# A hybrid decoder layer on one core: modulation blocks as plain fp32, GpSimd's products moved to VectorE, stores from two queues

## The chip, the core and the metric

The kernel runs on one core of one Trainium2 chip. Such a core has TensorE (matmuls), VectorE, ScalarE, GpSimd and SyncE, which here issues DMA transfers; the profile calls them PE, DVE, ACT, POOL and SP. The metric is the device time of one execution in microseconds, as the median of several runs.

## The reference, cut to what matters

One layer of a decoder trunk is applied to a prompt of 1024 tokens and to 8 single-token samples, with 1024 channels, all in fp32:

```python
mod = silu(c) @ w_ada + b_ada
shift, scale, gate = split(mod, 3)
h = rms_norm(x, norm_g) * (1 + scale) + shift
z = h @ w_in                      # 12 groups of columns, 3 branches
...                               # gated linear attention, short convolution, RG-LRU
out = (g1 * y_gla + g2 * y_sc + g3 * y_rg) @ w_out
x = x + gate * out
y = rms_norm(x, final_gain)
```

The layer also returns the new states of the three branches.

## The kernel before

Channels lie on the 128 partitions, in 8 tiles x0 to x7 of 1032 columns (two halves, each with 512 tokens and 4 samples). A large product is made from a split: `hi` is the operand in a reduced fp32 form (F32R), written by ScalarE, `lo` is the rest, which VectorE subtracts (`split`, L158), and three matmuls (hi hi, hi lo, lo hi) take the place of one. `product` (L336) makes seven block products where eight would be plain (`Pair`, `SEQ`), so the activations are kept in the combinations that `make_t` builds.

The beginning is a list of steps in the string `ORDER` (L36). Each name is a function and a number: X loads x, S squares it and adds to the sums of squares on TensorE, L loads a quarter of a modulation block from `w_ada`, R makes the norm factors (`group_rstd`), A multiplies a quarter (`ada_first`), E ends a block (`ada_end`: copy, transposes, `mod_ab`), N multiplies x by the norm factors (`norm_x`), H applies scale and shift (`make_h`), T makes the combinations and their splits (`make_t`), F multiplies one k of the first two products (`first_mm`), W and V load and split a small weight tile, Y and Z another one. Block j of the four modulation blocks gives scale and shift for x j and x j+4, which H, T and F of that j need.

Blocks 0, 2 and 3 are split, with 16 single matmuls for a block, and block 1 is plain fp32, with 8 (`EX`). The norms of x4 to x7 are on GpSimd (`POOL_J`). The affine step of the tokens is on VectorE for x0 to x3 (`AFF_V`) and on ScalarE for the others.

The order in the text is not the order on an engine. A list scheduler decides it when the program is compiled: of the instructions whose inputs and buffers it reckons to be ready, it queues the one that stands first in the text. The queues are then fixed, and an engine waits at the head of its queue. `tc.issue_after` in `ada_first` keeps TensorE's work for the later quarters behind the norm factors.

Then comes the long stream of 48 pairs of weight tiles, with the branches' work put between its matmuls, then the branch projections (`proj`) for three branches of 8 blocks, each with 48 matmuls for either half, and then the output projection with the final norm, in three parts of the columns (`part`: 388, 388 and 256 columns, each with 8 blocks f of 24 matmuls). For each f VectorE adds gate times product to x (L1206), ScalarE squares the sum (`fsq`, L1216) and VectorE adds the squares. At the end of a part a reciprocal root is made, four products scale the part (L1226), on GpSimd for the first two parts, and eight stores write it.

Buffers of 128 x 1032 come from two pools: `res` with 28 and `tmp` with 11. The splits of the merged activations, `mhi` and `mlo`, are in `res` for j below 6 and in `tmp` for 6 and 7. The weights of the output projection for f from 2 on are in `res` as well, as are the operands of the last branch's projection.

Of the kernel before, what the change touches and what calls it, by code (L numbers as in the profile page):

```python
# [7 lines left out]
F32R = mybir.dt.float32r  # L8
U32 = mybir.dt.uint32
AF = mybir.ActivationFunctionType  # L10
OP = mybir.AluOpType

P = 128
# [16 lines left out]
NSNAP = 5  # L30
WRAW, WSPL = 3, 5
AHEAD = 3
EX = (False, True, False, False)
ADA = ("res", "res", "res", "res")
FIRST_AFTER = (0, 2)
ORDER = (  # L36
# [3 lines left out]
AFF_V = (0, 1, 2, 3)  # L40
POOL_J = (4, 5, 6, 7)
RG_IDLE = (6, 1)
CHAIN = (4, 3)

# [32 lines left out]
def build(tc, a):  # L77
    nc = tc.nc
    from contextlib import ExitStack
    with ExitStack() as ctx:  # L80
# [8 lines left out]
        def bt(tag, name, dt=F32):  # L89
            return bigp.tile([P, TT], dt, name=name, tag=tag, bufs={"res": NRES, "tmp": NTMP}[tag])  # L90
# [19 lines left out]
        def tok(t):  # L110
            return hv(t)[:, :, :TH]
# [17 lines left out]
        vec, act, pe, gp, sp = nc.vector, nc.scalar, nc.tensor, nc.gpsimd, nc.sync  # L129
# [28 lines left out]
        def split(raw, hi, lo):  # L158
            act.activation(hi, raw, AF.Copy)  # L159
            vec.tensor_sub(lo, raw, hi.bitcast(F32))  # L160
# [33 lines left out]
        modA = ct([P, KT, 9], "modA")  # L194
# [5 lines left out]
        def ada_mm(blk, t, ws, i=None, kk=None):  # L200
            pg = ada_st[blk]
            m = 9 if len(ws) == 1 else 20
            for kk in range(2) if kk is None else (kk,):
                k = 2 * t + kk
                for i_ in range(len(ws)) if i is None else (i,):
                    c = csl if m == 9 else (c20, c20h)[i_]
                    pe.matmul(pg[:m], c[:, k, :], ws[i_][kk],  # L207
                              start=(k == 0 and i_ == 0), stop=(k == KT - 1 and i_ == len(ws) - 1))
# [3 lines left out]
        def ada_evac(blk, m):  # L212
            adar[blk] = tmp("adar")[:20, :512]
            act.activation(adar[blk][:m], ada_st[blk][:m], AF.Copy)

        def ada_tr(blk, m, i):
            pe.matmul(ada_st[blk][:, 9 * i:9 * i + 9], adar[blk][:m, i * P:(i + 1) * P], sel[:m], start=True, stop=True)
# [31 lines left out]
                              start=(k == 1 and g == 0), stop=(k == KT - 1 and g == 7))  # L249

        def norm_x(j):
            (gp if j in POOL_J else vec).tensor_mul(xt[j], xt[j], rs["rstd"])

        def make_h(j):
            x = xt[j]
            vec.tensor_mul(smp(x), smp(x), hs(modA[:, j, 1:9]))
            vec.tensor_add(smp(x), smp(x), hs(modB[:, j, 1:9]))
            if j in AFF_V:
                vec.tensor_scalar(tok(x), tok(x), modA[:, j, 0:1], modB[:, j, 0:1], op0=OP.mult, op1=OP.add)
            else:  # L260
                act.activation(tok(x), tok(x), AF.Identity, bias=modB[:, j, 0:1], scale=modA[:, j, 0:1])


        hop, b1a = {}, {}
# [17 lines left out]
                    hop[ids[i], k] = (half(hi, i), half(lo, i))  # L282

        def ada_load(blk, t):
            w = bt(ADA[blk], "wada")
            sp.dma_start(w[:, :1024], a["w_ada"][blk, t])
            raws[blk, t] = w[:, :1024]

        def ada_first(blk, t):
            if t == 0:  # L290
                ada_st[blk] = gpt("ada")
            raw = raws[blk, t]
            with ExitStack() as order:
                if (blk, t) >= FIRST_AFTER:
                    order.enter_context(tc.issue_after(rs["v"]))
                    order.enter_context(tc.issue_after(rs["p"]))
                if EX[blk]:
                    ws = (raw,)
                else:
                    ws = tuple(bt("res", f"ada{blk}_{t}{x}", F32R)[:, :1024] for x in "hl")  # L300
                    split(raw, *ws)
                ada_mm(blk, t, [(w[:, :512], w[:, 512:]) for w in ws])

        def ada_end(blk):
            m = 9 if EX[blk] else 20
            ada_evac(blk, m)
            for i in range(4):
                ada_tr(blk, m, i)
            mod_ab(ada_pt(blk), blk)

        def masks():
# [736 lines left out]
                loaded.add(n)  # L1048
                pairs[n].load()

        rg_consts()
        for q, (p, i) in enumerate(ops):
            n = q // 7
            if q % 7 == 0:
                load(n + 1)
            for d in range(1, AHEAD + 1):
                prep(q + d)
            if n or i not in (1, 2):
                p.mm(i)
            p.post(i)  # L1060
            if q % 7 == 6:
                after(*PAIRS[n])
# [78 lines left out]
        mhi, mlo = [], []  # L1141
        for br in range(3):
            nxt = []
            for j in range(8):
                g = tmp("gl")
                sp.dma_start(g, gs[br][j])
                for h, y in proj(a["wb"][br, j], [t[0] for t in u], [t[1] for t in u], f"y{br}_{j}"):
                    vec.tensor_mul(half(g, h), y, half(g, h))  # L1148
                if br:
                    p0 = tmp("p0")  # L1150
                    sp.dma_start(p0, pps[br - 1][j])
                    vec.tensor_add(g, g, p0)
                if br < 2:
                    sp.dma_start(pps[br][j], g)
                    nxt.append(load_u(br + 1, j, "tmp" if br == 0 and j >= 6 else "res"))
                else:
                    tag = "res" if j < 6 else "tmp"
                    mh, ml = bt(tag, f"mhi{j}", F32R), bt(tag, f"mlo{j}", F32R)
                    split(g, mh, ml)
                    mhi.append(mh)  # L1160
                    mlo.append(ml)
            u = nxt
# [13 lines left out]
        for ci in range(3):  # L1176
            w, wp = part(ci)[1:]

            def view(t):

                if ci == 2:
                    return hv(t)[:, :, :P]
                return part(ci)[0](t)

            def own(t):
                return hv2(t) if ci == 2 else t

            def hv2(t):
                return t.rearrange("p (h n) -> p h n", h=2)

            acc = tmp("facc")
            yp = []
            for f in range(8):
                ps = next_slot("wo_ps")
                o = ps[:, :w]
                for k in range(KT):
                    whi, wlo = (x[k // 4][:, k % 4 * P:(k % 4 + 1) * P] for x in wo[f])
                    for i, (m, x) in enumerate(((whi, mhi[k]), (whi, mlo[k]), (wlo, mhi[k]))):
                        pe.matmul(own(o), m, view(x), start=(k == 0 and i == 0), stop=(k == KT - 1 and i == 2))  # L1199
                if f % 2 == 0:  # L1200
                    yt = tmp("yt")[:, :2 * w].rearrange("p (f t) -> p f t", f=2)
                    for ff in range(2):
                        sp.dma_start(own(yt[:, ff]), view(a["x"][f + ff]))
                    yp.append(yt)
                y = yt[:, f % 2]
                vec.scalar_tensor_tensor(y[:, :wp], o[:, :wp], modG[:, f, 0:1], y[:, :wp], op0=OP.mult, op1=OP.add)  # L1206
                if wp < w:
                    t8 = sm([P, NS], "t8")
                    s0 = 1 + HS * (1 - ci)
                    vec.tensor_mul(t8[:, :HS], o[:, wp:], modG[:, f, s0:s0 + HS])  # L1210
                    vec.tensor_add(y[:, wp:w], y[:, wp:w], t8[:, :HS])  # L1211
                if f == 0:
                    act.activation(acc[:, :w], y, AF.Square)
                else:
                    sq = tmp("fsq")
                    act.activation(sq[:, :w], y, AF.Square)  # L1216
                    vec.tensor_add(acc[:, :w], acc[:, :w], sq[:, :w])
                act.activation(y, y, AF.Copy, scale=col("fgain", f))
            pg = gpt("fms")
            pe.matmul(pg[:, :w], ones_d, acc[:, :w], start=True, stop=True)  # L1220
            rst_ = tmp("frs")
            act.activation(rst_[:, :w], pg[:, :w], AF.Sqrt, bias=epsc)
            vec.reciprocal(rst_[:, :w], rst_[:, :w])  # L1223
            for f in range(0, 8, 2):
                y = yp[f // 2]
                (gp if ci < 2 else vec).tensor_mul(y, y, rst_[:, :w].unsqueeze(1).to_broadcast([P, 2, w]))  # L1226
                for ff in range(2):
                    sp.dma_start(view(a["o_y"][f + ff]), own(y[:, ff]))


def _ktile(w):
# [112 lines left out]
```

## Time and profile before

| | |
|---|---|
| device time, median of 3 runs | 1587.34 us (1586.84 to 1591.46) |
| profiled execution | 1590.05 us, with a span of 1588.2 us |
| TensorE busy | 1524.0 us |
| VectorE busy | 1048.2 us |
| ScalarE busy | 738.4 us |
| GpSimd busy | 31.6 us |
| mean granted clock of TensorE | 0.983 |

The profile is of one execution; its span runs from its first to its last instruction, and the device time lies a little above it. The granted clock is a share of full speed: it has two levels, 0.5 (1.2 GHz) and 1.0 (2.4 GHz), and a mean in between tells how long each was granted. A wait is named by who ended it.

### The profile page before, as it was taken

Reading aid. Unit: us, or ns where it says so; the run is one execution under the profiler, and the core shown is the slowest. Engines: PE = TensorE matmul, PEld = TensorE weight load, DVE = VectorE, ACT = ScalarE, POOL = GpSimd, SP = SyncE. Lnnn points to the kernel's source line nnn. Section 1 sums busy time; section 2 is a strip of 40 time slices with the busy share of each in tenths; the row PEclk is TensorE's granted clock in tenths of the full one; section 3 lists DMA queues with packets and bytes.
Section 4 is the critical chain, followed back from the end, with each engine's and each line's share of the span. In section 5 each row is a group of like instructions: output and inputs, shape, how many; then the busy total and the mean of one; then the engine's idle time right before and its main releaser. Section 6 shows DMA issues by size and latency. Waiting matters only on the chain.

```text
span 1588.2 us, 29025 instructions
## 1 busy us (share of the span) xinstructions
PE 1524.0 (96%) x12170; PEld 1485.4 (94%) x12170; DVE 1048.2 (66%) x1731; ACT 738.4 (46%) x1197; POOL 31.6 (2%) x27
## 2 busy tenths in 40 slices
PE   4899999999999999999999999999999999999995
PEld 3489999999999999999999999999999999999995
DVE  7887587695786966767776768676766434444543
ACT  5556356464473735445363545454544311112332
POOL 4000000000000000000000000000000000000011
PEclk8799999999999999999999999999999999999998
DMA  9011422223124122222112121312147666742223
GB/s 359 27 53 39 144 74 101 90 81 124 68 81 137 54 97 67 97 68 88 63 71 80 71 94 42 123 39 106 47 169 290 239 231 213 256 142 79 95 81 94
DMA packets 58145, 177.53 MB, mean 112 GB/s; under 512 B 7166, under 2 KB 17822, under 8 KB 58014
## 3 DMA queue, kind: packets, MB, share of 16 engines
q1 hardware_dynamic: 58014, 175.68, 31.6%
q8 instruction: 95, 1.56, 0.4%
q14 instruction: 36, 0.29, 0.1%
HBM read 132.64 MB, written 43.02 MB: 111 GB/s over the span
## 4 chain that ended last, share of the span: by engine, by line
PE 73%; DVE 14%; issue 5%; ACT 5%; DMA 1%; POOL 1%; POOLq 0%; DVEq 0%; ACTq 0%; SPq 0%
PE y_ps L1098 17%; PE m_c L342 8%; PE bs_c L342 6%; PE m_d L342 4%; PE rg_c L342 3%; PE ch_c L342 3%; PE gg_c L342 3%; PE qk_c L342 3%; PE bs_d L342 3%; PE wo_ps L1199 3%; DVE xc L856 2%; PE qk_d L342 2%; PE ada L207 2%; PE rg_d L342 1%; PE m_b L342 1%
## 5 line engine op out<-in xcount | busy, mean ns | idle before, releaser
L1098 PE MATMUL y_ps<-ul,y_h 128*128 128x256 f32 (+1 forms) x768 | 153.8, 282 | 0.5 <-DVE ul L160 0.5
L1098 PE MATMUL y_ps<-uh,y_l 128*128 128x256 f32 (+1 forms) x768 | 153.9, 282 | 0.0
L1098 PE MATMUL y_ps<-uh,y_h 128*128 128x256 f32 (+1 forms) x768 | 153.7, 282 | 0.0
L1098 PEld LDWEIGHTS y_ps<-ul,y_h 128*128 128x128 f32 x768 | 119.0, 188 | 1.6 <-DVE ul L160 0.9
L1098 PEld LDWEIGHTS y_ps<-uh,y_h 128*128 128x128 f32 x768 | 118.7, 188 | 0.8 <-ACT y_h L159 0.2
L1098 PEld LDWEIGHTS y_ps<-uh,y_l 128*128 128x128 f32 x768 | 118.7, 188 | 0.7
L159 ACT ACTIVATE y_h<-y_r 128x512 fp32r<-128x512 f32 x48 | 30.0, 629 | 131.6 <-PE y_ps L1098 120.6
L1148 DVE TENSOR_TENSOR gl<-y_ps,gl 128x516 f32<-128x516 f32 x48 | 33.2, 694 | 65.7 <-PE y_ps L1098 64.7
L1199 PE MATMUL wo_ps<-mhi,wo_h 128*128 128x388 f32 (+1 forms) x192 | 62.1, 324 | 3.5 <-DVE yt L1206 3.5
L160 DVE TENSOR_TENSOR y_l<-y_r,y_h 128x512 fp32r<-128x512 f32 x48 | 32.9, 688 | 48.0 <-ACT y_h L159 43.9
L1199 PE MATMUL wo_ps<-mlo,wo_h 128*128 128x388 f32 (+1 forms) x192 | 62.7, 327 | 0.3 <-DVE mlo L160 0.3
L1199 PE MATMUL wo_ps<-mhi,wo_l 128*128 128x388 f32 (+1 forms) x192 | 62.0, 323 | 0.0
L160 DVE TENSOR_TENSOR ul<-ul,uh 128x1032 fp32r<-128x1032 f32 x24 | 29.1, 1230 | 28.7 <-ACT uh L159 28.6
L159 ACT ACTIVATE uh<-ul 128x1032 fp32r<-128x1032 f32 x24 | 25.1, 1064 | 42.1 <-DMA ul<-us 36.1
L1226 POOL TENSOR_TENSOR yt<-yt,frs 128x776 f32<-128x776 f32 x8 | 14.6, 1860 | 1472.2 <-DVE frs L1223 1472.2
L1199 PEld LDWEIGHTS wo_ps<-mhi,wo_h 128*128 128x128 f32 x192 | 36.8, 192 | 3.9 <-DVE yt L1206 3.7
L1199 PEld LDWEIGHTS wo_ps<-mlo,wo_h 128*128 128x128 f32 x192 | 36.9, 192 | 0.9 <-DVE mlo L160 0.6
L1199 PEld LDWEIGHTS wo_ps<-mhi,wo_l 128*128 128x128 f32 x192 | 36.8, 192 | 0.3
L1216 ACT ACTIVATE fsq<-yt 128x388 f32<-128x388 f32 (+1 forms) x21 | 10.3, 491 | 53.3 <-DVE yt L1211 33.0
L1206 DVE SCALAR_TENSOR_TENSOR yt<-wo_ps,modG,yt 128x384 f32<-128x384 f32 (+1 forms) x24 | 13.4, 564 | 31.2 <-PE wo_ps L1199 25.1
L856 DVE SCALAR_TENSOR_TENSOR xc<-xp,pk,xc 128x1022 f32<-128x1022 f32 (+2 forms) x24 | 30.6, 1277 | 0.3
L908 ACT ACTIVATE rgt<-rgg,pk 128x344 f32<-128x344 f32 x48 | 24.0, 545 | 14.0 <-PE rgg L907 13.9
(2818 smaller groups left out, 5058.1 us busy)
## 6 DMA issues: line engine op xcount, KB each, us to landing
ul<-us SPq DMA_DIRECT2D x24, 516.0 KB, 5.7
gl<-gs SPq DMA_DIRECT2D x24, 516.0 KB, 4.8
y_r<-wb SPq DMA_DIRECT2D x24, 512.0 KB, 4.3
pps<-gl SPq DMA_DIRECT2D x16, 516.0 KB, 3.5
p<-pps SPq DMA_DIRECT2D x16, 516.0 KB, 5.6
wada<-w_ada SPq DMA_DIRECT2D x16, 512.0 KB, 10.2
gs<-ga SPq DMA_DIRECT2D x12, 516.0 KB, 2.6
gs<-gb SPq DMA_DIRECT2D x12, 516.0 KB, 2.6
```

The source lines that it names most:

```text
L159: act.activation(hi, raw, AF.Copy)
L160: vec.tensor_sub(lo, raw, hi.bitcast(F32))
L207: pe.matmul(pg[:m], c[:, k, :], ws[i_][kk], start=(k == 0 and i_ == 0), stop=(k == KT - 1 and i_ == len(ws) - 1))
L342: pe.matmul(pv(ps, c), m[:, k * P:(k + 1) * P], x[:, slice(*CHUNKS[c])], start=(first and k == 0 and n == 0), stop=(last and k == 3 and n ...
L856: vec.scalar_tensor_tensor(hv(out)[:, :, s:TH], hv(src)[:, :, :TH - s], w(i), hv(out)[:, :, s:TH], op0=OP.mult, op1=OP.add)
L908: act.activation(self.gate[i][:, cs], ps, AF.Sigmoid, bias=col(("rg_ba", "rg_bx")[i], self.n))
L1098: pe.matmul(pv(ps, c), m, half(x, h)[:, slice(*CHUNKS[c])], start=(k == 0 and i == 0), stop=(k == KT - 1 and i == 2))
L1148: vec.tensor_mul(half(g, h), y, half(g, h))
L1199: pe.matmul(own(o), m, view(x), start=(k == 0 and i == 0), stop=(k == KT - 1 and i == 2))
L1206: vec.scalar_tensor_tensor(y[:, :wp], o[:, :wp], modG[:, f, 0:1], y[:, :wp], op0=OP.mult, op1=OP.add)
L1216: act.activation(sq[:, :w], y, AF.Square)
L1226: (gp if ci < 2 else vec).tensor_mul(y, y, rst_[:, :w].unsqueeze(1).to_broadcast([P, 2, w]))
```

## The change

All four modulation blocks are multiplied as plain fp32, with no split (`EX` and the copies for `hi` and `lo` go). All norms are on VectorE, and all affine steps on ScalarE. `ORDER` is another one: block 3 is loaded with the others, the small weight tile is loaded earlier, two norms stand ahead of the end of each block, and T and F of one j stand between the blocks. `rg_consts` moves from ahead of the stream to its operation 70 in the text. `mhi` and `mlo` of j = 6 and 7 are in `res`. The final scaling is on VectorE in all three parts, and of the stores of each part every other one is issued by ScalarE.

```diff
-EX = (False, True, False, False)
-ADA = ("res", "res", "res", "res")
 FIRST_AFTER = (0, 2)
 ORDER = (
-    "X0 S0 X1 S1 X2 S2 X3 S3 X4 S4 X5 S5 X6 S6 X7 S7 L00 L01 L02 L03 L10 L11 L12 L13 L20 L21 L22 "
-    "L23 R A00 A01 A02 A03 E0 A10 A11 A12 A13 E1 W0 V0 L30 L31 L32 L33 N0 H0 N4 H4 T0 F0 A20 A21 "
-    "A22 A23 E2 N1 H1 N5 H5 T1 F1 A30 A31 A32 A33 E3 N2 H2 N6 H6 T2 F2 N3 H3 N7 H7 T3 F3 Y Z")
-AFF_V = (0, 1, 2, 3)
-POOL_J = (4, 5, 6, 7)
+    "X0 S0 X1 S1 X2 S2 X3 S3 X4 S4 X5 S5 X6 S6 X7 S7 L00 L01 L02 L03 W0 L10 L11 L12 L13 L20 L21 L22 L23 L30 L31 "
+    "L32 L33 R A00 A01 A02 A03 N0 N4 E0 H0 H4 V0 T0 N1 N5 F0 A10 A11 A12 A13 E1 H1 H5 T1 N2 N6 F1 A20 A21 A22 A23 "
+    "E2 H2 H6 T2 N3 N7 F2 A30 A31 A32 A33 E3 H3 H7 T3 F3 Y Z")
...
         def norm_x(j):
-            (gp if j in POOL_J else vec).tensor_mul(xt[j], xt[j], rs["rstd"])
+            vec.tensor_mul(xt[j], xt[j], rs["rstd"])
...
-            if j in AFF_V:
-                vec.tensor_scalar(tok(x), tok(x), modA[:, j, 0:1], modB[:, j, 0:1], op0=OP.mult, op1=OP.add)
-            else:
-                act.activation(tok(x), tok(x), AF.Identity, bias=modB[:, j, 0:1], scale=modA[:, j, 0:1])
+            act.activation(tok(x), tok(x), AF.Identity, bias=modB[:, j, 0:1], scale=modA[:, j, 0:1])
...
-                if EX[blk]:
-                    ws = (raw,)
-                else:
-                    ws = tuple(bt("res", f"ada{blk}_{t}{x}", F32R)[:, :1024] for x in "hl")
-                    split(raw, *ws)
-                ada_mm(blk, t, [(w[:, :512], w[:, 512:]) for w in ws])
+                ada_mm(blk, t, [(raw[:, :512], raw[:, 512:])])
...
-        rg_consts()
         for q, (p, i) in enumerate(ops):
             n = q // 7
+            if q == 70:
+                rg_consts()
...
-                    tag = "res" if j < 6 else "tmp"
-                    mh, ml = bt(tag, f"mhi{j}", F32R), bt(tag, f"mlo{j}", F32R)
+                    mh, ml = bt("res", f"mhi{j}", F32R), bt("res", f"mlo{j}", F32R)
...
-                (gp if ci < 2 else vec).tensor_mul(y, y, rst_[:, :w].unsqueeze(1).to_broadcast([P, 2, w]))
+                vec.tensor_mul(y, y, rst_[:, :w].unsqueeze(1).to_broadcast([P, 2, w]))
                 for ff in range(2):
-                    sp.dma_start(view(a["o_y"][f + ff]), own(y[:, ff]))
+                    (sp if ff else act).dma_start(view(a["o_y"][f + ff]), own(y[:, ff]))
```

## Rows read from the trace of the kernel before

**Rows 1.** The page, busy time by engine: us, share of the span, instructions.

```profile
...
PE 1524.0 (96%) x12170; PEld 1485.4 (94%) x12170; DVE 1048.2 (66%) x1731; ACT 738.4 (46%) x1197; POOL 31.6 (2%) x27
...
```

**Rows 2.** Windows: stretch, length, busy us (PE, PEld, DVE, ACT, POOL), clock, DMA, GB/s.

```profile
...
24.40:95.10 70.70, 51.77 (x224) 29.92 (x224) 65.14 (x97) 39.39 (x51) 14.35 (x5) 0.78 0.28 103
95.10:145.10 50.00, 48.27 (x389) 47.81 (x390) 36.12 (x79) 28.23 (x51) 0.00 (x0) 0.97 0.19 64
...
```

**Rows 3.** Timeline of VectorE and GpSimd from 24 us: start, us, instruction.

```profile
...
25.61 3.40 DVE L160 TENSOR_TENSOR ada_0l<-wada,ada_0h 128x1024 fp32r<-128x1024 f32 x1
...
39.24 3.51 DVE L252 TENSOR_TENSOR x<-x,rstd 128x1032 f32<-128x1032 f32 x3
...
24.50 13.40 POOL L252 TENSOR_TENSOR x<-x,rstd 128x1032 f32<-128x1032 f32 x4 [19.70 <-ACT rstd L333]
...
```

**Rows 4.** Waits from 1480 us: who waited for whom, us, times, longest.

```profile
...
ACT fsq L1216 <- POOL yt L1226: 10.4, 2, 6.1
...
PE wo_ps L1199 <- DVE yt L1206: 3.5, 1, 3.5
...
```

**Rows 5.** Groups of VectorE, shapes apart, 24 to 96: busy us, mean ns.

```profile
...
L160 DVE TENSOR_TENSOR t34l<-t,t34h 128x1032 fp32r<-128x1032 f32 x4 | 4.9, 1226 | 0.0
...
L259 DVE TENSOR_SCALAR x<-x,modA,modB 128x1024 f32<-128x1024 f32 x4 | 3.2, 805 | 0.0
...
L272 DVE TENSOR_TENSOR t<-x,t 128x516 f32<-128x516 f32 x4 | 2.8, 688 | 0.0
...
L227 DVE TENSOR_TENSOR modB<-ada,pk 128x18 f32<-128x18 f32 x4 | 0.7, 177 | 5.4 <-PE ada L217 5.4
...
```

**Rows 6.** Timeline of TensorE in the first 115 us.

```profile
...
10.80 9.41 PE L248 MATMUL ms_ps<-sq,mk 128*128 128x129 f32 x64 [10.80 <-DVE sq L244]
21.77 2.02 PE L331 MATMUL rs_ps<-rg,sk 128*128 128x129 f32 x16 [1.55 <-DVE rg L326]
...
40.44 1.88 PE L207 MATMUL ada<-wada,csl 128*9 128x512 f32 x2
42.24 1.08 PE L217 MATMUL ada<-sel,adar 20*128 20x9 f32 x8
43.26 5.32 PE L207 MATMUL ada<-wada,csl 128*9 128x512 f32 x12
...
95.12 0.51 PE L342 MATMUL qk_c<-t12h,qk0w_h 128*128 128x256 f32 x2 [1.91 <-ACT qk0s L375]
...
```

**Rows 7.** Timeline of TensorE behind its last gap.

```profile
...
1564.61 0.56 PE L1199 MATMUL wo_ps<-mhi,wo_h 128*128 128x256 f32 x1 [3.47 <-DVE yt L1206]
...
1568.14 0.28 PE L1199 MATMUL wo_ps<-mlo,wo_h 128*128 128x256 f32 x1
1568.26 0.28 PE L1199 MATMUL wo_ps<-mhi,wo_l 128*128 128x256 f32 x1
...
```

**Rows 8.** Groups of ScalarE, 24 to 96 us.

```profile
...
L261 ACT ACTIVATE x<-x,modB,modA 128x1024 f32<-128x1024 f32 x4 | 5.0, 1242 | 7.5 <-DVE modA L229 4.1 <-DVE rcs L875 3.3
...
L159 ACT ACTIVATE ada_1h<-wada 128x1024 fp32r<-128x1024 f32 x3 | 3.1, 1045 | 0.0
...
```

**Rows 9.** SyncE's queue, and DMA issues to 45 us (last: us to landing).

```profile
...
9.09 14.36 SPq L286 DMA_DIRECT2D wada<-w_ada  x12
...
wada<-w_ada SPq DMA_DIRECT2D x16, 512.0 KB, 10.2
...
```

**Rows 10.** Timeline of VectorE near the stream's start.

```profile
...
92.90 0.17 DVE L965 COPY scs<-sst 128x8 f32<-128x8 f32 x1
...
```

**Rows 11.** Timelines of GpSimd, VectorE and SyncE's queue; landing of `o_y`.

```profile
...
1518.24 7.31 POOL L1226 TENSOR_TENSOR yt<-yt,frs 128x776 f32<-128x776 f32 x4 [1445.19 <-DVE frs L1223]
...
1579.46 2.50 DVE L1226 TENSOR_TENSOR yt<-yt,frs 128x512 f32<-128x512 f32 x4
...
1580.18 5.26 SPq L1228 DMA_DIRECT2D o_y<-yt  x8
...
DMA to landing us min/median/max: 1.9/2.1/3.0
...
```

More of the change, by code (lines that the diff above doesn't have):

```diff
@@ L284, in ada_load @@
         def ada_load(blk, t):
-            w = bt(ADA[blk], "wada")
+            w = bt("res", "wada")
             sp.dma_start(w[:, :1024], a["w_ada"][blk, t])
@@ L296, in ada_first @@
                     order.enter_context(tc.issue_after(rs["p"]))
-                if EX[blk]:
-                    ws = (raw,)
-                else:
-                    ws = tuple(bt("res", f"ada{blk}_{t}{x}", F32R)[:, :1024] for x in "hl")
-                    split(raw, *ws)
-                ada_mm(blk, t, [(w[:, :512], w[:, 512:]) for w in ws])
+                ada_mm(blk, t, [(raw[:, :512], raw[:, 512:])])
         def ada_end(blk):
-            m = 9 if EX[blk] else 20
-            ada_evac(blk, m)
+            ada_evac(blk, 9)
             for i in range(4):
-                ada_tr(blk, m, i)
+                ada_tr(blk, 9, i)
             mod_ab(ada_pt(blk), blk)
```

## The prediction

> **What bounds the kernel now.** I read the page first, then the windows of the beginning and of the end, then each engine's timeline there, and last the waits. The page says that TensorE is busy 96% of the span [rows 1]; the reader should take from it that only the two ends, where TensorE is not full, can give anything. The windows show where: from 24.4 us, when the norm factors are ready, to 95.1 us, when the long unbroken stream of `product` matmuls begins, TensorE is busy 51.8 of 70.7 us at a mean clock of 0.78, while VectorE is busy 65.1 [rows 2]. In the 50 us after that TensorE has 48.3 and VectorE only 36.1. So the beginning is a VectorE stage, and every microsecond by which the stream starts earlier should reach the end of the kernel, since nothing in the stream depends on the clock on the wall.
>
> The timelines show why VectorE is that late. GpSimd's four norms take 13.40 us from 24.50, and in just that stretch the `lo` split of a modulation tile takes VectorE 3.40 us, where the three norms at 39.24 take 3.51 together [rows 3]. Instructions in a row overlap by some 0.08 us (3.51 against three times 1.22).
>
> At the other end, 3.47 us of TensorE are lost in one gap, and the waits put it behind `fsq`, which waits for GpSimd's last products [rows 4].
>
> **The change, part by part: VectorE in the beginning.** Twelve `lo` splits go (three blocks of four tiles): four slow ones at 3.40 - 0.08 = 3.32, together 13.3, and eight at 1.22 - 0.08 = 1.14, together 9.1 (the 128x1032 `t34l` is the nearest row, 1226 ns) [rows 3, 5]. Four affine steps of L259 go to ScalarE: 4 x 0.73 = 2.9 [rows 5]. Four norms come from GpSimd: 4 x 1.14 = 4.6 more. Net: 13.3 + 9.1 + 2.9 - 4.6 = 20.7 less. VectorE then has 65.1 - 20.7 = 44.4 us of work in place of 65.1, and idled 5.6 of its 70.7, nearly all of it (5.4) waiting for the transposes of a modulation block [rows 2, 5]. With the same idle time the stream starts at 24.4 + 44.4 + 5.6 = 74.4 us.
>
> **TensorE in the beginning.** This is what speaks against the change. A block as plain fp32 is eight matmuls, recorded as 16. Twelve records took 5.32 us at full clock, 0.44 each, so 7.0 a block; two took 1.88 at the lower level, 0.94 each, so 15.0 a block [rows 6]. Counted from 20.2, where the sums of squares end, TensorE has four blocks (28.0), the spreading of the factors (2.0), four groups of transposes (4 x 1.0) and `first_mm` for k = 0 and 1 (20 matmuls each at 0.12, 2.4) before the last block ends: 38.8, so 59.0 [rows 6, 7]. Behind that come the copy, the transposes' tail and the three small VectorE steps, some 1.5, one affine step of 1.24 on ScalarE [rows 8], and the last `make_t` to the stream, which I put at 8.3: four half-size differences at 0.6, one half split at 0.6 and three full ones at 1.14 make 6.4, plus 1.9 for `zst` and the first copy (the gap ahead of the stream, 1.91) [rows 5, 6]. That gives 70.0. So TensorE's chain and VectorE's ledger lie within 5 us of each other, which means that neither hides the other's delays well. I take 74 us, the VectorE sum, because its idle time stands for just such mutual waiting: **the stream starts 21 us earlier**. The bounds: with no idle time VectorE ends at 68.8, a gain of 26; if the first two tiles' matmuls (8 x 0.44 = 3.5) stand ahead of the spreading of the factors, which has 1.55 us of slack, everything starts 2 us later and the gain is 19.
>
> The loads do not bound this. Twelve tiles are issued in 14.36 us and take 10.2 to land [rows 9]; at that pace (1.2 to 1.3 us a tile) sixteen in a row from 9.1 have landed near 39, while the fourth block is not reached before some 50. Block 3 is loaded ahead of the factors now; its tiles and the eight squares together fit the 28 `res` buffers (2 masks + 8 + 16 = 26).
>
> ScalarE loses 12 `hi` splits of 1.05 and gains four affine steps of 1.24, so it has less to do than before [rows 8]. `rg_consts` moves to operation 70 in the text, but the order on the engines is by readiness: a copy of line 965, which belongs to a much later pair, ran at 92.90 [rows 10]. I cost it at nothing; if it did run late, some 30 instructions of 0.17 on VectorE would lie beside the stream, where VectorE has 14 us free in 50 [rows 2].
>
> **The end.** `mhi6`, `mlo6`, `mhi7`, `mlo7` leave the eleven `tmp` buffers, so the last stage has eleven instead of seven. The wait of `fsq` on GpSimd's product has then no cause, and the 3.47 us gap goes [rows 4]. With it goes the drop of the clock behind it: sixteen matmuls started between 1564.61 and 1568.14, 3.53 us, where the next ones stand 0.12 apart, so 1.9; 1.6 more [rows 7]. In return the four must wait for a `res` buffer until the last half of the last `proj` has read its first operands for the last time (6 matmuls, 0.7 us, into its 48, 5.8 us). The first two are wanted at k = 6 of the first output block, 5.1 + 18 x 0.18 = 8.3 us later (0.18 is 0.12 for 388 columns in place of 256), and splitting them takes 2.3: covered. The last two are made after that `proj` in any case.
>
> The products of the first two parts come to VectorE: two bursts of four. GpSimd took 7.31 for four [rows 11]; VectorE takes 0.61 for 512 columns and 1.14 for 1032, so about 0.88 for 776, 3.5 a burst. Behind the reciprocal (2.5) that holds `yt` up for 6 us. TensorE has three PSUM slots of at least 24 x 0.12 = 2.9 us each: covered.
>
> **Last stores.** Now eight issues in a row take 5.26 us, 0.66 each, and the products feed two stores every 0.61 [rows 11]. With two queues, each has four: 1580.18 + 4 x 0.66 = 1582.8 in place of 1585.4, so 2.6; the landing of 2.1 stays. I take 2.4, with bounds of 0 (the transfers, not their issue, set the end) and 2.6. By the Trainium skill (DMA: Bandwidth & Descriptors, Issuing engines are not separate DMA queues) all queues share the same DMA engines and a second one saves only the issue time, usually small beside the transfer; if it is small here too, the term is near 0 and the time 2.4 higher, 1561.4. The row contradicts "small" for these stores: 5.26 of issue against 2.1 to land.
>
> **Sum.** 21 + 3.5 + 1.6 + 2.4 = 28.5. The profiled execution took 1590.05 us, 1.85 more than its span, so 1561.5; the median of the runs is 2.7 below it, so **1559 us**. About 0.3% (5 us) is what a measurement here can tell from no change.
>
> **Rivals.**
> - *The lower clock over the long blocks.* In 24.4 to 95.1 the mean clock was 0.78 [rows 2], because TensorE had gaps. In the changed order a block is always at hand while VectorE works, which speaks against it; `first_mm` standing in the queue ahead of a ready block speaks for it. Each block at the lower level costs 8.0; two of them 16: 1575. Chance 0.16.
> - *The end gives nothing*: stores issued on ScalarE wait for VectorE's products with the squares queued behind them, and take over the part of GpSimd. Then 7.5 is missing: 1566. Three PSUM slots speak against it. Chance 0.08.
> - *The change does not do what it says*: the order of waits, block by block, stays as it was, and only the slowed splits (4 x 2.18 = 8.7) are saved there. 1559 + 12.3 = 1571. The idle time of only 5.6 us speaks against it. Chance 0.06.
> - *Slower*: TensorE at the lower level through the whole beginning. Its 38.8 us double, the stream starts at 74 + 39 = 113, and the time is 1598. It ends the gain once 28.5 of the 38.8 are paid, so with about three blocks and a half at that level. The first half of this stage had such a clock, but with TensorE idle for most of it. Chance 0.05.
> - The forecast: 0.65, with its own range 1553 (26 + 5 + 2.6 saved) to 1567 (one block at the lower level).
>
> Faster by over 0.3%: 0.91; within 0.3%: 0.04 (the tops of the first and third rivals, a part of the fourth); slower: 0.05. The range 1552 to 1576 takes in the forecast, two slow blocks and a lost end, and leaves out the slower case and what lies beyond these bounds.
>
> **What would show it.** Right: no VectorE instruction of 3 us near 30 us; the 16 plain matmuls of each block 0.44 apart; the first unbroken `qk_c` group near 74; no gap of TensorE above 1 us after 1480; stores ending less than 6 us after the first product of the last part. Wrong: plain matmuls 0.94 apart for more than a block, TensorE waiting in `first_mm` for `b2l` with a block ready behind it, or a gap in the last part that ends on a store.

## The result, and the profile after

The changed kernel takes 1566.27 us, the median of three runs (1565.74 to 1570.33). One far slower execution of either kernel (2113 and 8385 us) is left out. The ratio to the kernel before is 0.987, 95% interval 0.983 to 0.990: 21.1 us, or 1.3%, faster, where 28.3 were forecast. The profiled execution took 1565.74 us with a span of 1563.8, where before's had 1590.05 and 1588.2, so 24.4 us of span are to be found.

The windows of the kernel after, cut where the norm factors were ready before and where the stream of `product` matmuls now begins (stretch, length, busy us and count of PE, PEld, DVE, ACT and POOL, clock, DMA share, GB/s):

```profile
...
24.40:78.26 53.86, 49.57 (x220) 26.18 (x218) 44.46 (x87) 33.25 (x44) 0.95 (x1) 0.97 0.36 136
78.26:128.26 50.00, 48.27 (x403) 47.81 (x404) 37.48 (x81) 29.47 (x53) 0.00 (x0) 1.00 0.18 64
...
```

The stream begins at 78.26, not 95.12: 16.9 of the 24.4 us. VectorE's work in the stretch is 44.46 us, but it lies in 53.86, so it idled 9.4 us, where it had idled 5.6 of 70.7 [rows 2]. The second row tells of a part for which the prediction has no term: its 50 us hold 403 matmuls at a clock of 1.00, those of before 389 at 0.97. At 0.12 us each, 14 matmuls are 1.7 us. This isn't the chance of one execution. In the five profiles with the beginning of the kernel before (its own and those of the four runs on the end), these 50 us have 389 or 390 matmuls at 0.97; in the two with the beginning of the kernel after (its own and that of the run with half the bytes), 403 at 1.00. In the kernel before the clock falls behind a gap of 1.71 us of TensorE, 38 us into the stream; the kernel after has the same gap (1.72 us) and keeps the full clock. Why it does isn't shown.

VectorE's timeline in that stretch (start, us, instruction, idle time before it and what ended that):

```profile
...
20.83 0.96 DVE L313 RECIPROCAL rg<-rg 128x129 f32<-128x129 f32 x1 [0.71 <-ACT rg L312]
31.38 0.18 DVE L223 TENSOR_TENSOR modB<-ada,pk 128x18 f32<-128x18 f32 x1 [9.59 <-PE ada L213]
...
31.77 2.37 DVE L248 TENSOR_TENSOR x<-x,rstd 128x1032 f32<-128x1032 f32 x2
...
45.93 0.18 DVE L223 TENSOR_TENSOR modB<-ada,pk 128x18 f32<-128x18 f32 x1 [2.28 <-PE ada L213]
...
```

No instruction of 3 us is left near 30 us [rows 3]. In their place stand two waits for the transposes of a block. Of the first, 6.98 us lie behind 24.40; with the second they make 9.3 of the 9.4 us. Why the two norms at 31.77 did not fill the first wait is seen in the queue of ScalarE:

```profile
...
29.47 0.59 ACT L210 ACTIVATE adar<-ada 9x512 f32<-9x512 f32 x1 [8.67 <-PE ada L203]
29.96 1.05 ACT L320 ACTIVATE rstd<-rs_ps 128x516 f32<-128x516 f32 x2
...
```

The copies that make `rstd` ran at 22.93 before; now they stand behind the copy of block 0, which waited for the whole block. TensorE's timeline shows why the second wait is long:

```profile
...
22.13 2.05 PE L318 MATMUL rs_ps<-rg,sk 128*128 128x129 f32 x16
24.11 6.17 PE L203 MATMUL ada<-wada,csl 128*9 128x512 f32 x14
30.22 1.05 PE L213 MATMUL ada<-sel,adar 9*128 9x9 f32 x8
31.20 13.04 PE L203 MATMUL ada<-wada,csl 128*9 128x512 f32 x30
...
44.84 1.05 PE L213 MATMUL ada<-sel,adar 9*128 9x9 f32 x8
...
78.26 0.51 PE L329 MATMUL qk_c<-t12h,qk0w_h 128*128 128x256 f32 x2 [1.92 <-ACT qk0s L362]
...
```

Records stand 0.435 apart, and the last row is the stream's first. Of the fourteen at 24.11, twelve are the rest of block 0 (its copy began at 29.47) and two are of block 1. The thirty that run in a row from 31.20 are the other fourteen of block 1 and all sixteen of block 2. Only behind them come block 1's transposes at 44.84, though block 1 was done near 31.20 + 14 x 0.435 = 37.3.

At the end, the gap of 3.47 us [rows 7] is 1.03:

```profile
...
1542.64 0.39 PE L1186 MATMUL wo_ps<-mhi,wo_h 128*128 128x256 f32 x1 [1.03 <-DVE yt L1193]
1542.86 0.28 PE L1186 MATMUL wo_ps<-mlo,wo_h 128*128 128x256 f32 x1
...
```

Matmuls stand 0.12 apart behind it, so the clock held. What is left of the gap is a load, as SyncE's queue and VectorE's timeline show:

```profile
...
1534.05 3.00 SPq L1215 DMA_DIRECT2D o_y<-yt  x4
1537.10 4.47 SPq L1190 DMA_DIRECT2D yt<-x  x6
...
1542.10 0.92 DVE L1193 SCALAR_TENSOR_TENSOR yt<-wo_ps,modG,yt 128x256 f32<-128x256 f32 x2 [4.07 <-DMA yt<-x]
...
1555.96 2.50 DVE L1213 TENSOR_TENSOR yt<-yt,frs 128x512 f32<-128x512 f32 x4
1556.69 2.66 ACTq L1215 DMA_DIRECT2D o_y<-yt  x4
1556.72 3.04 SPq L1215 DMA_DIRECT2D o_y<-yt  x4
...
```

The `yt` loads are issued behind the stores. The last stores are issued in 3.0 us on two queues, where one took 5.26 [rows 11]; yet from the first of the last products to the end of the span it is 7.84 us, against 8.74: 0.9 less. From the end of the last `proj` to the end of the span the kernel after is 5.5 us shorter (105.9 against 111.4).

So the 24.4 us are 16.9 (start of the stream) + 5.5 (last part, stores included) + 2.0 (the stream, 1.7 of it from its first 50 us).

### The profile page after: what moved, and what is told of

Its sections match the earlier page's. It is cut to its first block, busy times and chain, and to the rows that moved or that the text cites. A ratio compares the mean times of both kernels' runs of the same rounds, so it can differ in the third digit from the quotient of the medians.

```text
span 1563.8 us, 28956 instructions
## 1 busy us (share of the span) xinstructions
PE 1521.6 (97%) x12170; PEld 1480.2 (95%) x12170; DVE 1033.0 (66%) x1727; ACT 730.4 (47%) x1189; POOL 3.6 (0%) x15
## 4 chain that ended last, share of the span: by engine, by line
PE 77%; DVE 13%; ACT 5%; issue 4%; DMA 0%; DVEq 0%; SPq 0%; ACTq 0%
PE y_ps L1086 18%; PE m_c L329 8%; PE bs_c L329 6%; PE wo_ps L1186 5%; PE m_d L329 4%; PE ch_c L329 4%; PE rg_c L329 3%; PE gg_c L329 3%; PE qk_c L329 3%; PE bs_d L329 3%; DVE xc L843 2%; PE ada L203 2%; PE qk_d L329 2%; PE rg_d L329 2%; PE m_b L329 1%
## 5 line engine op out<-in xcount | busy, mean ns | idle before, releaser
L688 ACT ACTIVATE vt<-po 128x128 f32<-128x128 f32 x64 | 14.2, 276 | 31.8 <-PE po L686 31.8
```

Source lines behind the costliest of these rows:

```text
L688: act.activation(hd["o"][d][:, gcols(g)], po[:, d * P:(d + 1) * P], AF.Copy)
```

## The experiments

Each was run beside the kernel before on the same chip. Where a single execution stands for a kernel, its profile is read by stages, not by its total.

**GpSimd's norms alone.** The kernel before, with

```
-POOL_J = (4, 5, 6, 7)
+POOL_J = ()
```

> The kernel before with one edit: all eight norms on VectorE, GpSimd without work in the beginning. Theory (GpSimd's norms slow VectorE's splits): the four splits near 26 us fall from 3.40 to about 1.22 us each, 8.7 us saved, four norms of 1.14 added, so the stream starts about 4 us earlier, near 91. Rival (the slow splits have another cause, and only the plain blocks bring the gain): the splits stay at 3.4, the norms come on top, and the stream starts near 99.7.

As the theory had it, the stream began at 90.66 (span 1581.9; the end is untouched). The four splits that followed the first norm took 1.22 us each instead of 3.4:

```profile
...
25.76 1.22 DVE L160 TENSOR_TENSOR ada_0l<-wada,ada_0h 128x1024 fp32r<-128x1024 f32 x1
26.90 1.22 DVE L160 TENSOR_TENSOR ada_1l<-wada,ada_1h 128x1024 fp32r<-128x1024 f32 x1
...
```

The splits are the same and only GpSimd is idle beside them, so it was GpSimd that made them slow, and four norms more on VectorE cost less than that.

**Plain blocks alone.** The kernel before, with

```
-EX = (False, True, False, False)
+EX = (True, True, True, True)
```

> The kernel before with one edit: all four modulation blocks as plain fp32, with its own step order, GpSimd's norms and the end as they were. Theory (the gain is VectorE work that goes): twelve splits go, 22.4 us, and up to 6.6 come back because VectorE's own four norms now run beside GpSimd's; the stream starts between 73 and 80. Rival (the new step order makes the gain): without it the stream starts after 85.

The stream began at 84.19 (span 1576.4), between the two and nearer the rival. VectorE was busy 49.18 us of the 59.79, so the theory's sum of work held (65.1 - 22.4 + 6.6 = 49.3); what it lacked were the 10.6 us of idle time. The missing splits did not end the contention; it moved to whatever VectorE did beside GpSimd's four norms:

```profile
...
31.67 1.82 DVE L229 TENSOR_TENSOR modA<-modA,pk 128x18 f32<-128x18 f32 x1
33.41 1.22 DVE L252 TENSOR_TENSOR x<-x,rstd 128x1032 f32<-128x1032 f32 x1
34.55 2.58 DVE L427 TENSOR_TENSOR wlr<-first_r,wlr 128x256 fp32r<-128x256 f32 x1
37.06 2.33 DVE L256 TENSOR_TENSOR x<-x,modA 128x8 f32<-128x8 f32 x1
39.31 2.92 DVE L259 TENSOR_SCALAR x<-x,modA,modB 128x1024 f32<-128x1024 f32 x1
...
31.09 10.59 POOL L252 TENSOR_TENSOR x<-x,rstd 128x1032 f32<-128x1032 f32 x4 [26.29 <-ACT rstd L333]
...
```

Plain blocks alone gave 10.9 us, no work on GpSimd alone 4.5, all edits of the beginning 16.9. The new step order and the affine steps on ScalarE were not run by themselves, so their share isn't shown.

**The three edits of the end**, together and one by one, on the kernel before. Together:

```
-                    tag = "res" if j < 6 else "tmp"
-                    mh, ml = bt(tag, f"mhi{j}", F32R), bt(tag, f"mlo{j}", F32R)
+                    mh, ml = bt("res", f"mhi{j}", F32R), bt("res", f"mlo{j}", F32R)
...
-                (gp if ci < 2 else vec).tensor_mul(y, y, rst_...)
+                vec.tensor_mul(y, y, rst_...)
...
-                    sp.dma_start(view(a["o_y"][f + ff]), own(y[:, ff]))
+                    (sp if ff else act).dma_start(view(a["o_y"][f + ff]), own(y[:, ff]))
```

> The kernel before with the three edits of the end alone (the four split tiles in the larger pool, the scaling on VectorE, stores from two queues). Theory: TensorE's gap in the last part falls from 3.47 to about 1.0 us, its clock does not drop behind it, and the last stores save 0.9; the end from the first output matmul is 5.5 us shorter, span near 1582.7, with the beginning unchanged (stream at 95.1). Rival (the end gains only because it is reached in another phase): gap and span as before.

Only the buffers:

> The kernel before with one edit of the end: the splits of the last two pairs take buffers of the tag res alone. Theory (the gap of 3.47 us ahead of wo_ps comes from GpSimd's scaling, which holds the order of VectorE's work, not from these buffers): the gap stays at 3 to 3.5 us, the span at 1586 to 1588.5. Rival (the two splits wait for buffers of the tag tmp, which the scaling's tiles hold): the gap falls under 1.5 us, the span by 2 or more.

Only the scaling on VectorE:

> The kernel before with one edit of the end: all scaling on VectorE. Theory (the gap comes from GpSimd's scaling, 7.3 us for four products where VectorE takes about 3.5): the gap falls to about 1 us and the clock stays at full behind it, 2.4 + 1.6 = 4 us off the span (1584), the end after the first last product unchanged at 8.0. Rival (the yt loads, queued on SP behind the stores, end the gap, whoever scales): the gap stays at 2.5 us or more, under 1.5 us off the span.

Only the two queues:

> The kernel before with one edit of the end: stores from the queues of SP and ScalarE in turn. Theory (the last eight stores were bound by one queue's issue, 5.26 us, and become bound by the transfer, 8 x 128 KB in 3.7 us): the last products to the end of the span 7.2 where it was 8.05, and with the middle stores no longer in one row on SP the gap changes by less than 0.5: 0.5 to 1.5 us off the span. Rival (the gap is the yt loads' place on SP behind the stores): the gap falls by 1 us or more too, 2 or more off the span.

Counted from the end of the last `proj`, so that the beginning plays no part (us):

| kernel | to the end of the span | gap | first last product to the end of the span |
|---|---|---|---|
| before | 111.37 | 3.47 | 8.74 |
| buffers alone | 110.33 | 3.24 | 8.58 |
| two queues alone | 109.05 | 2.81 | 7.51 |
| scaling alone | 106.71 | 1.06 | 8.59 |
| all three | 106.08 | 1.13 | 7.90 |

The scaling alone takes the gap down to 1.06, as the theory of that run had it; the buffers do nothing for it. The end of the kernel before also stands unchanged in the runs with GpSimd's norms alone and with plain blocks alone: 110.9 and 111.4 us, gaps of 2.87 and 2.98. So single executions of that end differ by 0.6 in the gap and by 0.5 in the time, and neither the 0.7 that two queues take off the gap nor half of the 1.0 of the buffers can be told from nothing. The rival of two queues wanted at least 1 us off the gap and did not come true; their 2.3 in all is more than their theory's 1.5. The three don't add up (1.0 + 2.3 + 4.7 = 8.0 against 5.3): they shorten the same gap and the same stores, and each carries that difference between executions.

The gap ends on a load in every one of these runs. SyncE's queue, ScalarE's `fsq` and VectorE's addition behind the gap, in the kernel before:

```profile
...
1554.44 6.25 SPq L1228 DMA_DIRECT2D o_y<-yt  x8
1560.79 6.75 SPq L1203 DMA_DIRECT2D yt<-x  x6
...
1564.07 0.89 DVE L1206 SCALAR_TENSOR_TENSOR yt<-wo_ps,modG,yt 128x256 f32<-128x256 f32 x2 [3.32 <-DMA yt<-x]
...
```

With the buffers alone:

```profile
...
1551.06 0.40 ACT L1215 ACTIVATE fsq<-yt 128x256 f32<-128x256 f32 x1
...
1558.47 3.83 SPq L1202 DMA_DIRECT2D yt<-x  x6
...
1561.31 0.90 DVE L1205 SCALAR_TENSOR_TENSOR yt<-wo_ps,modG,yt 128x256 f32<-128x256 f32 x2 [9.23 <-DMA yt<-x]
...
```

With the scaling alone:

```profile
...
1554.91 7.60 SPq L1203 DMA_DIRECT2D yt<-x  x6
...
1559.05 0.87 DVE L1206 SCALAR_TENSOR_TENSOR yt<-wo_ps,modG,yt 128x256 f32<-128x256 f32 x2 [4.13 <-DMA yt<-x]
...
```

With the buffers alone the wait of `fsq` for GpSimd [rows 4] is gone: the one at 1551.06 starts without idle time. The gap stays, because the addition now waits 9.23 us for its `yt` loads. These stand on SyncE's queue behind the eight stores of the part before, and each store waits for its scaled product. From the end of the reciprocal to the addition it is 11.60 us in the kernel before, 11.45 with the buffers alone and 9.25 with the scaling on VectorE: the 2.35 us are those by which the gap is shorter (2.41). So GpSimd's scaling makes the gap by way of the stores and the loads behind them. That path is read from the traces; no run moves the loads alone.

**Half the bytes of the last stores.** The kernel after, with the rows of 64 of the 128 partitions left out of the last part's output:

```
+                    h_ = slice(0, 64 if ci == 2 else P)
-                    (sp if ff else act).dma_start(view(a["o_y"][f + ff]), own(y[:, ff]))
+                    (sp if ff else act).dma_start(view(a["o_y"][f + ff])[h_], own(y[:, ff])[h_])
```

> The kernel after with the last eight stores cut to half: 64 of the 128 partitions are stored, the rest of the last part's output is left out. Theory (with two queues these stores are bound by the transfer, 8 x 128 KB at some 285 GB/s): the end from the first last product falls from 7.16 to 5.3 (5.0 to 5.8). Rival (bound by the issues, 0.66 to 0.76 us each on a queue, or by the time to land): 6.5 or more.

The expectation counts to the landing of the last store, 0.68 before the end of the span. Counted to the end of the span it is 6.35 where the kernel after has 7.84, so 1.5 less; as the expectation counts, 5.7, inside its theory's range. The issues still took 2.94 and 2.60 us. Windows of the kernel after and of this run over the stretch in which the stores move:

```profile
...
1557.90:1561.70 3.80, 0.00 (x0) 0.00 (x0) 0.56 (x1) 0.00 (x0) 0.00 (x0) 0.50 0.95 275
...
```

```profile
...
1558.70:1561.50 2.80, 0.00 (x0) 0.00 (x0) 0.45 (x1) 0.00 (x0) 0.00 (x0) 0.50 0.81 183
...
```

With all bytes the DMA engines are busy 0.95 of the 3.8 us, and fewer bytes end sooner: with two queues the transfer is the bound. Half the bytes don't take half the time, and the DMA engines are busy 0.81 there; what bounds that case isn't shown.

**The norm factors first.** The kernel after, with the copies to `rstd` ahead of block 0's copy in ScalarE's queue:

```
-                act.activation(half(rstd, s), ps[...], AF.Copy)
+                rs["c"] = act.activation(half(rstd, s), ps[...], AF.Copy).ins
...
-            ada_evac(blk, 9)
+            with tc.issue_after(rs["c"]):
+                ada_evac(blk, 9)
```

> The changed kernel with one edit: on ScalarE the two copies of the norm factors are queued ahead of the copy of modulation block 0. Theory (VectorE stands idle for 7 us from 24.4 because the factors wait in ScalarE's queue behind that copy): factors ready near 24.8 instead of 31.0, VectorE's norms start there, the stream starts 3 to 4 us earlier than 78.3, near 75. Rival (the transposes of block 1, which stand behind block 2 on TensorE, decide): the norms start earlier, but the stream stays within 1 us of 78.3.

My theory fell. The factors came at 23.24 and the norms at 24.76, and the stream at 79.83, later than the rival's bound too: the scheduler put twelve of block 1's records ahead of block 0's transposes, and VectorE waited for these instead. TensorE's timeline and VectorE's:

```profile
...
24.02 12.18 PE L203 MATMUL ada<-wada,csl 128*9 128x512 f32 x28
36.14 1.05 PE L213 MATMUL ada<-sel,adar 9*128 9x9 f32 x8
...
24.76 2.38 DVE L248 TENSOR_TENSOR x<-x,rstd 128x1032 f32<-128x1032 f32 x2 [3.06 <-ACT rstd L321]
37.30 0.18 DVE L223 TENSOR_TENSOR modB<-ada,pk 128x18 f32<-128x18 f32 x1 [10.16 <-PE ada L213]
...
```

**And the transposes ahead of the next block.** As before, and

```
+            rs["t", blk] = pe.matmul(ada_st[blk][...], adar[blk][...], sel[:m], start=True, stop=True).ins
...
+                if blk and t:
+                    order.enter_context(tc.issue_after(rs["t", blk - 1]))
```

> The kernel after, with the norm factors copied on ScalarE ahead of block 0's copy, and each block's transposes ahead of the next block's later matmuls on TensorE. Theory (VectorE's idle time of 9.4 us is two waits: for the factors and block 0's transposes, and 2.28 us for block 1's transposes behind block 2's 30 records): the two norms of 2.37 us fill the first wait and the second is gone, so 2.37 + 2.28 = 4.65 us less, the first modulation tile still near 31, the second near 41, the stream at 78.26 - 4.65 = 73.6 (72.5 to 75), the span near 1559.2. Rival (another wait takes the place of these, on block loads or on ScalarE's affine steps): the stream at 77 or later, the span within 1.3 of 1563.8.

The theory fell again: the stream at 80.05, ratio to before 0.987 (0.985 to 0.989). The modulation tiles came at 32.47 and 40.32, near where it had them, but VectorE still waited 5.01 us for block 0's transposes, and now also 3.12 us for `t12h` on ScalarE, and ScalarE for the load of `rgw`, whose split stood in its queue ahead:

```profile
...
32.47 0.18 DVE L223 TENSOR_TENSOR modB<-ada,pk 128x18 f32<-128x18 f32 x1 [5.01 <-PE ada L213]
...
44.85 1.23 DVE L156 TENSOR_TENSOR t12l<-t,t12h 128x1032 fp32r<-128x1032 f32 x1 [3.12 <-ACT t12h L155]
...
43.45 0.42 ACT L155 ACTIVATE rgwh<-rgw 128x256 fp32r<-128x256 f32 x1 [3.50 <-DMA rgw<-rg_wax]
...
```

**All eight norms ahead of the first modulation tile**, on top of this, and without the edit on the transposes:

```
-... N0 N4 E0 H0 H4 V0 T0 N1 N5 F0 ... T1 N2 N6 F1 ... T2 N3 N7 F2
+... N0 N4 N1 N5 N2 N6 N3 N7 E0 H0 H4 V0 T0 F0 ... T1 F1 ... T2 F2
```

> The kernel with the factors' copies and the transposes in front, and all eight norms ahead of the first modulation tile on VectorE. Theory (VectorE's ledger decides, and its waits are covered when it has norms to do: for block 0's transposes 5.01 us, and 3.12 us for a split on ScalarE behind the rgw load that lands at 43.4): the first modulation tile at 25.1 + 8 x 1.15 = 34.3, no idle time over 1 us up to 45, the stream at 80.05 - 8.1 = 72 (71 to 73.5), the span near 1561. Rival 1 (TensorE decides: full from 20 to 45, and 28.86 of 35 us busy behind that): the stream at 80.05 - 6.1 = 74 at the earliest, 74 to 77, with TensorE full until it starts. Rival 2 (the loads, at 400 GB/s until 42 us, decide): the stream at 78.5 or later.

> The kernel with the factors' copies in front and all eight norms ahead of the first modulation tile, the transposes as in the kernel after. Theory (with six more norms in hand VectorE hardly feels block 0's transposes behind block 1, 37.3 in the run with the copies alone): 37.3 - 34.3 = 3 us of idle time where it was 10.2, the stream at 79.8 - 6.9 = 73 (72 to 75). Rival (the later modulation tiles, with their transposes behind the next block, set the stream): 77 or later.

Both theories missed by far: the streams began at 85.40 and 85.19, the ratios to before were 0.989 (0.987 to 0.990) and 0.988 (0.987 to 0.990). The norms did fill VectorE (in the first of the two, the first tile at 34.04), but with the order of the text changed the scheduler put the split of `rgw` ahead of ScalarE's affine steps, and the first difference of `qk0` ahead of VectorE's next work. ScalarE's and VectorE's timelines in the first of the two:

```profile
...
29.99 1.04 ACT L415 ACTIVATE wlr<-first_r 128x1024 fp32r<-128x1024 f32 x1
42.94 0.42 ACT L155 ACTIVATE rgwh<-rgw 128x256 fp32r<-128x256 f32 x1 [11.90 <-DMA rgw<-rg_wax]
...
41.64 0.69 DVE L354 TENSOR_TENSOR qk0s<-qk0a_r,qk0b_r 128x512 f32<-128x512 f32 x1 [6.93 <-DMA qk0b_r<-wz]
...
```

The last rival of either run has the number (78.5 or later, 77 or later). But the load of `rgw` is no later than in the kernel after, whose split of it ran at 43.62; what changed is the place of the work on two loads, at the head of two queues.

**The work on late loads behind the first group.** As the first of these two, and the split of `rgw`, the differences of `qk0` and the copies to `rcs` and `scs` are issued behind the first group's `t34` splits, each in this way:

```
-                split(wr, *self.w)
+                with tc.issue_after(rs["s", 0, "t34"][0]):
+                    split(wr, *self.w)
```

> The kernel of the run with eight norms and the transposes in front, and all work that waits for a late load (the rgw split on ScalarE, the qk0 differences and the rcs and scs copies on VectorE) put behind the first group's splits. Theory (what moved that run's stream to 85.4 was ScalarE's 11.9 us of waiting for the rgw load with the affine steps queued behind it, and VectorE's 6.9 us for qk0b_r; with these gone the norms fill VectorE's early waits): the first group's differences near 37, the second's near 46 (51.1 in the kernel after), and then block 3, whose matmuls TensorE finishes at 62, sets the last group: the stream at 74 to 76.5, the span 1560 to 1563. Rival (the beginning has another queue of this kind, whatever is put in front): the stream at 78 or later.

Here the theory held: the groups at 35.83 and 45.87, the last tile at 64.48, the stream at 75.35. Windows:

```profile
...
24.40:75.35 50.95, 48.14 (x220) 24.54 (x218) 45.34 (x95) 32.25 (x43) 0.95 (x1) 1.00 0.38 146
75.35:125.35 50.00, 48.36 (x388) 47.89 (x389) 35.31 (x69) 27.98 (x50) 0.00 (x0) 0.97 0.18 64
...
```

VectorE idled 5.6 us of 50.95, TensorE 2.8. The span, 1563.6, is that of the kernel after all the same, just past the expected 1563: the stream's first 50 us had 388 matmuls at a clock of 0.97 here and 403 at 1.00 there, which is 1.8 of the 2.9 us by which it began earlier. The median was 1566.3, the ratio to before 0.984 (0.983 to 0.986). It lies below the change's 0.987, but the intervals overlap, so that it beats the changed kernel is not shown.

## Why the prediction was right, point by point

- **VectorE's work.** 44.4 us forecast, 44.46 measured. The prices of the removed and added instructions held as a sum, and the run with GpSimd's norms alone shows that the slow splits fall from 3.4 to 1.2 us when GpSimd is idle.
- **The step that failed: "With the same idle time the stream starts at 24.4 + 44.4 + 5.6 = 74.4 us."** The idle time was 9.4, and the stream began at 78.26: 16.9 earlier, not 21. The splits of block 0 were what VectorE did while it waited for block 0; with them gone the wait stood open, and the work that could have filled it (norms) was tied behind ScalarE's copy of the same block. The experiments name what kept the wait open: places in three in-order queues (the `rstd` copies, the transposes, the work on late loads). With all of them moved and the norms in front, 24.4 + 45.3 + 5.6 = 75.3 was measured; that these 5.6 us equal the forecast's is chance, for they are other waits. Moving the first alone, or the first two, gave nothing, and with the norms put in front as well the stream came later still: each time the next place in a queue took over. Which of the three moves the last run could do without is not settled.
- **TensorE.** A plain record took 0.43 to 0.44 at full clock as forecast, and the clock in the beginning rose from 0.78 to 0.97. The two rivals on the lower clock did not come true: a block was always at hand, and TensorE was busy without a break from 20 to 45 us.
- **The gap**, 3.5 + 1.6 forecast: the whole last part gave 5.5 with 0.9 of it at the stores, so 4.6 here. The size nearly held, the path did not. The prediction closed the gap by the buffers: with eleven of them the wait of `fsq` for GpSimd's product "has then no cause". With the buffers alone that wait went, and the gap stayed at 3.24. What ended it before and after were the `yt` loads behind the stores on SyncE's queue, which GpSimd's products held up; the scaling on VectorE, which the prediction counted only as a cost that is covered, took the gap to 1.06. The 1.0 us that stays, on the same loads, was not foreseen.
- **Last stores**, 2.4 forecast: 0.9. The mechanism was right (one queue's issue was the bound), the size was wrong, because the transfer is next: 8 x 128 KB at some 285 GB/s are 3.7 us, against 5.26 of issue. The rule of the Trainium skill (DMA: Bandwidth & Descriptors, Issuing engines are not separate DMA queues) was nearer than I allowed: the engines behind both queues are the same, and at 0.95 busy they bound the stores once the issue was halved.
- **`rg_consts`** cost nothing, as forecast: its steps ran between 2 and 9.5 us in both kernels, so the move in the text moved nothing on the engine.
- **The signs it named.** Two came: no VectorE instruction of 3 us near 30 us, and plain records 0.44 apart. Three were missed: the first unbroken group at 78.26 and not near 74, a gap of 1.03 where none above 1 was to be left, and last stores that land 7.2 us after the first product and not under 6.
- **What made up for it, and luck.** Terms short by 4.1 + 0.5 + 1.5 = 6.1 of 28.5 leave 22.4; the stream's own 2.0, for which there was no term, makes 24.4 of span. The medians are only 21.1 apart, because the profiled execution of before lay 2.7 above its median and that of after 0.5 below. That 1566.27 still lies inside the forecast's own range is partly luck: its upper end, 1567, was the price of a block at the lower clock, which did not happen.

## What to carry to other kernels

Work that is removed from the busiest engine may have been covering a wait: before counting it as time, look what the engine waited for before and after it, and what is ready to take its place. When a stage's order is made from readiness, ask of each in-order queue what stands behind an instruction that waits for a whole block or a late load; repairing one such place was worth nothing here while the next was as late. A wait that a view names may not be the one that binds: one of them went with the buffers, and the gap stayed. Two queues for stores gained here down to the transfer time and no further.

## What the runs showed of the hardware that was not expected

- **A tiny VectorE instruction can take as long as GpSimd's large one.** Beside GpSimd's norms of 2.65 us each, a product of 128x8 took 2.33 us (0.16 alone), a 128x256 difference 2.58 (0.42), the affine step 2.92 (0.80). The Trainium skill (SBUF — State Buffer, Who interferes with whom) says that a VectorE instruction with two inputs in SBUF shares a read port with a GpSimd instruction that reads SBUF, and that the later one waits for the whole of the earlier one. The rows with two inputs agree: each lost 2.2 us, whatever its own size, as the splits of the kernel before did (3.40 against 1.22 [rows 3]), a little less than the 2.65 us of a GpSimd instruction. The affine step, which lost 2.1, reads one tensor and two columns of scalars, and of such an instruction that sentence says nothing. Not everything in the stretch was held up: the norm at 33.41 took 1.22.
- **The clock rises and falls differently between executions of the same instructions.** In the run with two queues alone, whose beginning is that of the kernel before, TensorE's clock rose later:

```profile
...
42.39 1.87 PE L217 MATMUL ada<-sel,adar 20*128 20x9 f32 x8
44.19 7.35 PE L207 MATMUL ada<-wada,csl 128*9 128x512 f32 x12
...
```

  The same transposes took 1.08 and the same twelve records 5.32 before [rows 6], and the stream began at 98.67, where the four other profiles with this beginning have 95.12 to 95.82. The 100 us from 400 us behind the stream's start had 754 matmuls at a granted clock of 0.97 in the kernel before and 776 at 1.00 in the run with the scaling alone, whose text is the same up to the last part. A comparison of two single profiles of this kernel carries such steps, here 2.6 us (22 matmuls at 0.12) and 3.5 us.
